# A quarter token tile moved from dense products to gathers, a whole tile likewise, and the reordering of background work that goes with it

## The chip, the cores and the metric

The kernel runs on one core of one Trainium2 chip. The metric is the device time of one execution in microseconds (us); the smaller, the better. Before the change three runs gave 3330.73, 3334.25 and 3336.74 us, median 3334.25 us.

## What is computed

One decoder block over 1024 tokens of width 1024, in float32. The first sub-layer (pooling mixer and forgetting attention, gated) is not touched. The second one is a product-key mixture of 16384 single-neuron experts; its reference, cut to what matters:

```python
q = einsum('bsd,dk->bsk', h, w_query)            # 8 heads, two halves of 128
s1, i1 = top_k(scores of half 0, 16); s2, i2 = top_k(scores of half 1, 16)
top_s, sel = top_k(s1[..., :, None] + s2[..., None, :], 16)
idx = (i1 * 128 + i2)[sel]; gates = softmax(top_s)   # 8 x 16 experts a token
a = gelu(einsum('cd,chkd->chk', x, expert_u[idx])) * gates
out = einsum('chk,chkd->cd', a, expert_v[idx])
```

Each token so uses 128 of the 16384 experts: 128 rows of `expert_u` and 128 rows of `expert_v`, 1024 floats each.

## The kernel before

The 1024 tokens are eight tiles of 128. The first sub-layer, the query products and the top-k of the halves run in three phases of 512, 256 and 256 tokens (`PHASES`, L26; `phase`, L481). In each phase TensorE (PE) has a stream of matmuls, and `tick` (L62) lets a list of background generators (`bg["todo"]`) advance beside it: each matmul group earns credit in us times a rate (`RATES`, L41), and each `yield` of a generator costs what it says.

The experts are done in two ways.

- **Dense** (tiles 1 to 5, `DT0`, `DT1`, L27): all 16384 experts are computed for these 640 tokens. `choose` (L810) finds a token's 128 experts and gates on VectorE (DVE); `gates` (L943) spreads them into a full matrix of gates in DRAM, with one-hot products on PE (`G`, L985) in 32 steps a tile; `dense_experts` (L1002) then runs over 16 groups of 1024 experts. In a group, eight `up` steps (L1018) make 128 experts each for two halves of `NH` = 320 tokens, 24 matmuls a half (8 slices of the width times three, `mm3`, L278, high and low parts of the operands); Gelu, times the gates, split into `ah` and `al`. Eight `down` steps (L1037) multiply by `expert_v` in the same way and add into `accT`. So the stage has 16 x 16 weights of 512 KB. Each is loaded on SP's queue into `wr` (two buffers), rounded to `wh` on ScalarE (ACT) and its remainder `wl` is made on GpSimd (POOL) (`load_w`, L242). There are three `wh`/`wl` pairs in this stage (`W["n"]` = 2 and `W["m"]` = 1).
- **Gathered** (tiles 0, 6 and 7, `experts`, L907): 128 indirect DMAs from POOL fetch, for each of the 128 tokens on the partitions, row k of `expert_u` (512 KB a gather); DVE makes the dot products (L917). Then 128 gathers of `expert_v`, which DVE adds with their weights into `acc` (L927). The operands `h2` and `acc` are in PSUM. Five buffers `g` go round (`g_row`, L894). These generators run in the background of the dense stage, each gather costing `GSTEP` = 1.46 of credit. What is left when the products end is emitted by `drain()` (L1088).

The kernel is not run in the order of its text: the tile framework replays it against its own model of time and writes each engine's list of instructions (`schedule_with_timeline_sim`, L1190). On the chip each engine and queue then runs its list in order. The gathers stay in order among themselves (`keep_in_program_order`, L904).

Of the kernel before, what the change touches and what calls it, by code (L numbers as in the profile page):

```python
# [17 lines left out]
D = 1024  # L18
# [8 lines left out]
DT0, DT1 = 1, 6  # L27
ND = (DT1 - DT0) * 128
# [12 lines left out]
RATES = (0.92, 0.95, 0.74, 0.95)  # L41
# [5 lines left out]
def block_kernel(ctx: ExitStack, tc: tile.TileContext, I, out, dbg=None):  # L47
# [173 lines left out]
    def rstd(ss):  # L221
        nc.vector.tensor_add(ss[:, 2:3], ss[:, 0:1], ss[:, 1:2])
        nc.scalar.activation(ss[:, 3:4], ss[:, 2:3], AF.Sqrt, scale=1.0 / D, bias=epsc)
        nc.vector.reciprocal(ss[:, 3:4], ss[:, 3:4])
        return ss[:, 3:4]
# [166 lines left out]
    def head2(c):  # L392
# [17 lines left out]
        fhl = c.big.tile([48, n], R, name="fhl", tag="fhl", bufs=1)  # L410
# [70 lines left out]
    def phase(c, nxt):  # L481
# [230 lines left out]
        if p == 2:  # L712
            bg["todo"].insert(0, gates(W["gb"], DT1 - 1))
# [32 lines left out]
        dl = [i for i in range(NQ) if DT0 <= qb0 + i < DT1]  # L746
        gl = [i for i in range(NQ) if i not in dl]
        if dl:
            T = slice(dl[0] * 128, dl[-1] * 128 + 128)
            o = (qb0 + dl[0] - DT0) * 128  # L750
            mv(h2dT[0][:, :, o:o + len(dl) * 128], h2h[:, :, T])
            mv(h2dT[1][:, :, o:o + len(dl) * 128], h2l[:, :, T])
            per = D // n
            for b, v in enumerate(tiles):
                mv(x1dT[:, b * per:(b + 1) * per, o:o + len(dl) * 128], v[:, :, T])
# [54 lines left out]
    def choose(tt, mv_, mx_):  # L810
        yield 0.0
        dense = DT0 <= tt < DT1
# [54 lines left out]
        gt = sel.tile([128, PH, 16], F, name="gate", tag="gated" if dense else f"gate{tt}", bufs=1)  # L867
# [7 lines left out]
        if not dense or (dbg and "idx" in dbg):  # L875
            ix = sel.tile([128, 128], I32, name=f"idx{tt}")
# [4 lines left out]
        if dense:  # L881
            tr = W["gb"].tile([128, 3, 128], F, name="pairT", tag="pairT", bufs=DT1 - DT0)
# [5 lines left out]
        if dbg and "idx" in dbg:  # L888
            nc.sync.dma_start(dbg["idx"][tt * 128:(tt + 1) * 128], ix)
            nc.sync.dma_start(dbg["gate"][tt * 128:(tt + 1) * 128], gate[tt])  # L890

    X = {"i": 0, "p": None}
# [13 lines left out]

    def experts(tt):  # L907
        yield 0.0
        row = g_row("row")
        nc.sync.dma_start(row, h2d[tt])  # L910
        h2 = X["ps"].tile([128, D], F, name="h2", tag="gx", bufs=1)
        nc.scalar.activation(h2, row, AF.Copy)
        dots = gp.tile([128, 128], F, name="dots", tag="dots", bufs=1)
# [5 lines left out]
        nc.vector.tensor_mul(dots, dots, gate[tt])  # L919
        acc = X["ps"].tile([128, D], F, name="acc", tag="gx", bufs=1)  # L920
        for k in range(128):
            yield GSTEP
            g = gather(I["peer_v"], idx[tt][:, k:k + 1])
# [8 lines left out]
        r1, r2 = g_row("r1"), g_row("r2")  # L932
        nc.sync.dma_start(r1, x1d[tt])
        nc.sync.dma_start(r2, I["final_g"].partition_broadcast(128))
        nc.vector.tensor_tensor(r0, r0, r1, op=OP.add)
        ss = cst.tile([128, 4], F, name="ss", tag="ssg", bufs=2)
        nc.scalar.activation(r1, r0, AF.Square, accum_out=ss[:, 3:4])
        nc.scalar.activation(ss[:, 3:4], ss[:, 3:4], AF.Sqrt, scale=1.0 / D, bias=epsc)
        nc.vector.reciprocal(ss[:, 3:4], ss[:, 3:4])
        nc.vector.scalar_tensor_tensor(r0, r0, ss[:, 3:4], r2, op0=OP.mult, op1=OP.mult)  # L940
        nc.sync.dma_start(out[tt * 128:(tt + 1) * 128, :], r0)

    def gates(gb, tt):  # L943
# [35 lines left out]
        def use(q, o1, o2):  # L979
# [8 lines left out]
            if r == 3:  # L988
                nc.sync.dma_start(Gd[:, :, (tt - DT0) * 8 + c, :].rearrange("g p x -> p g x"),
# [3 lines left out]
        for q in range(32):  # L993
# [8 lines left out]
    def dense_experts():  # L1002
# [3 lines left out]
        W["x"], W["m"], W["i"] = dd, 1, 2  # L1006
# [78 lines left out]
        for i in range(DT1 - DT0):  # L1085
            finish_dense(i, rows, fg[:, 0])
# [107 lines left out]
```

## Time and profile before

| what | us |
|---|---|
| median of three runs | 3334.25 |
| the profiled execution, its own time | 3331.02 |
| its span, first to last instruction | 3329.3 |
| PE busy in the span | 3123.0 |
| DVE busy | 2440.7 |
| POOL busy | 1754.0 |
| ACT busy | 1266.9 |

The mean granted clock of TensorE was 0.977 of full speed. All times below are from the start of the span. The dense stage begins at about 1490 us and its last product ends at about 3312 us; the three phases lie before it. PE's busy time is a sum over overlapping matmuls that is cut to their union, so a busy PE may still issue more slowly than it could; the pace of matmuls in a stretch is its length over their number.

### The profile page before, as it was taken

How to read it: one execution, taken by the hardware profiler on the slowest of the kernel's cores; microseconds unless marked ns; L12 is line 12 of the kernel's file. 1: busy time of each engine (PE TensorE's matmuls, PEld its weight loads, DVE VectorE, ACT ScalarE, POOL GpSimd, SP SyncE). 2: the span in 40 equal slices, each digit the busy share in tenths (PEclk: the TensorE clock that was granted, in tenths of full speed). 3: DMA queues.
4: the chain of work that ended last, by engine and by line, in shares of the span. 5: the costliest groups of instructions: out<-in, count | busy, mean ns of one | idle time of the engine just before them, and what ended most of it. 6: DMA issues, size and time to landing. Idle time of an engine off the chain costs nothing.

```text
span 3329.3 us, 56918 instructions
## 1 busy us (share of the span) xinstructions
PE 3123.0 (94%) x20912; PEld 2982.7 (90%) x20912; DVE 2440.7 (73%) x5520; ACT 1266.9 (38%) x2405; POOL 1754.0 (53%) x1328
## 2 busy tenths in 40 slices
PE   6999889888888899889999999999999999999998
PEld 4778778778778889789999999999999999999998
DVE  5764557998947987669977877686778767767774
ACT  4555543346542666532222322332232222222222
POOL 1233233014411323326677777687778767877782
PEclk9999999899999999999999999999999999999999
DMA  8987787777788778888899999899999989999994
GB/s 321 354 300 260 274 290 285 243 228 232 235 280 301 234 254 280 274 315 310 278 343 348 329 331 339 312 349 336 333 337 335 335 318 348 335 336 337 348 323 149
DMA packets 379990, 1004.60 MB, mean 302 GB/s; under 512 B 34896, under 2 KB 147136, under 8 KB 379584
## 3 DMA queue, kind: packets, MB, share of 16 engines
q1 hardware_dynamic: 269120, 598.26, 52.3%
q0 software_dynamic: 110592, 402.70, 33.1%
q8 instruction: 166, 2.72, 0.3%
q14 instruction: 112, 0.92, 0.1%
HBM read 851.25 MB, written 149.58 MB: 301 GB/s over the span
## 4 chain that ended last, share of the span: by engine, by line
PE 59%; DVE 11%; DMA 3%; ACT 1%; issue 1%; POOL 0%; SPq 0%; DVEq 0%; ACTq 0%; POOLq 0%
PE z L281 10%; PE z L279 10%; PE z L280 10%; PE oT L280 8%; PE oT L279 8%; PE oT L281 8%; PE G L985 3%; DVE g L917 2%; DVE cand L860 1%; DVE o L975 1%; DMA wl<-w_queryl 1%; DVE pk L864 1%; DMA wr<-w_queryl 1%; DVE mx L585 1%; ACT Gb L986 1%
## 5 line engine op out<-in xcount | busy, mean ns | idle before, releaser
L233 POOL TENSOR_TENSOR wl<-wr,wh 128x1024 fp32r<-128x1024 f32 x320 | 777.0, 2429 | 550.4 <-ACT wh L232 510.2
L232 ACT ACTIVATE wh<-wr 128x1024 fp32r<-128x1024 f32 x325 | 344.0, 1059 | 973.4 <-PE oT L280 429.5
L279 PE MATMUL z<-h2x,wh 128*128 128x320 f32 x2048 | 636.4, 311 | 7.7 <-DVE al L233 5.8
L281 PE MATMUL z<-h2x,wl 128*128 128x320 f32 x2048 | 635.5, 311 | 3.1 <-POOL wl L233 3.1
L280 PE MATMUL z<-h2x,wh 128*128 128x320 f32 x2048 | 635.6, 310 | 0.0
L280 PE MATMUL oT<-al,wh 128*128 128x320 f32 x2048 | 632.8, 309 | 0.4 <-DVE al L233 0.3
L279 PE MATMUL oT<-ah,wh 128*128 128x320 f32 x2048 | 631.9, 310 | 0.7 <-ACT ah L232 0.7
L281 PE MATMUL oT<-ah,wl 128*128 128x320 f32 x2048 | 632.3, 309 | 0.2 <-POOL wl L233 0.2
L917 DVE SCALAR_TENSOR_TENSOR g<-g,h 128x1024 f32<-128x1024 f32 x384 | 461.0, 1215 | 77.5 <-DMA g<-peer_u,idx 75.9
L927 DVE SCALAR_TENSOR_TENSOR acc<-g,dots,acc 128x1024 f32<-128x1024 f32 x381 | 489.2, 1284 | 22.6 <-DMA g<-peer_v,idx 18.8
L902 POOL DMA_INDIRECT g<-peer_u,idx x384 | 363.2, 946 | 163.3 <-DVE g L917 70.3
L902 POOL DMA_INDIRECT g<-peer_v,idx x384 | 361.3, 941 | 114.8 <-issue 50.5
L279 PEld LDWEIGHTS z<-h2x,wh 128*128 128x128 f32 x2048 | 386.6, 189 | 8.9 <-DVE al L233 6.6
L281 PEld LDWEIGHTS z<-h2x,wl 128*128 128x128 f32 x2048 | 386.3, 189 | 3.5 <-POOL wl L233 3.5
L280 PEld LDWEIGHTS z<-h2x,wh 128*128 128x128 f32 x2048 | 386.5, 189 | 0.0
L279 PEld LDWEIGHTS oT<-ah,wh 128*128 128x128 f32 x2048 | 384.1, 188 | 1.4 <-ACT ah L232 1.3
L280 PEld LDWEIGHTS oT<-al,wh 128*128 128x128 f32 x2048 | 384.4, 188 | 0.9 <-DVE al L233 0.9
L281 PEld LDWEIGHTS oT<-ah,wl 128*128 128x128 f32 x2048 | 384.3, 188 | 0.5 <-POOL wl L233 0.5
L973 POOL TENSOR_TENSOR o<-hi,lo 128x512 f32<-128x512 f32 x160 | 199.9, 1252 | 300.0 <-PE G L985 245.4
L279 PE MATMUL z<-hTh,wh 128*128 128x256 f32 (+1 forms) x840 | 290.2, 350 | 29.6 <-issue 12.3
L1050 DVE TENSOR_TENSOR accT<-accT,oT 128x320 f32<-128x320 f32 x240 | 116.5, 487 | 233.6 <-PE oT L281 232.8
L280 PE MATMUL z<-hTl,wh 128*128 128x256 f32 (+1 forms) x840 | 285.0, 339 | 1.3 <-DVE hTl L233 1.3
(286 smaller groups left out, 6094.5 us busy)
## 6 DMA issues: line engine op xcount, KB each, us to landing
wr<-ut SPq DMA_DIRECT2D x128, 512.0 KB
wr<-vt SPq DMA_DIRECT2D x128, 512.0 KB
Gd<-Gb SPq DMA_DIRECT2D x40, 1024.0 KB
Gg<-Gd SPq DMA_DIRECT2D x64, 640.0 KB
wh<-w_inh SPq DMA_DIRECT2D x60, 512.0 KB
wl<-w_inl SPq DMA_DIRECT2D x60, 512.0 KB
wm<-w_mod SPq DMA_DIRECT2D x48, 512.0 KB
wr<-w_in SPq DMA_DIRECT2D x45, 512.0 KB
```

Of the source, the lines that this page charges most:

```text
L232: nc.scalar.activation(hi, src, AF.Copy)
L233: eng_lo.tensor_tensor(lo, src, hi.bitcast(F), op=OP.subtract)
L279: nc.tensor.matmul(ps, ah, bh, start=start, stop=False)
L280: nc.tensor.matmul(ps, ah, bl, start=False, stop=False)
L281: nc.tensor.matmul(ps, al, bh, start=False, stop=stop)
L585: nc.vector.tensor_reduce(mx[:, x:x + 1], sp[:, :w], axis=AX.X, op=OP.max, negate=True)
L902: d = nc.gpsimd.indirect_dma_start(out=g, out_offset=None, in_=table, in_offset=bass.IndirectOffsetOnAxis(ap=col, axis=0))
L917: nc.vector.scalar_tensor_tensor(g, g, 1.0, h2, op0=OP.mult, op1=OP.mult, accum_out=dots[:, k:k + 1])
L927: nc.vector.scalar_tensor_tensor(acc, g, dots[:, k:k + 1], acc, op0=OP.mult, op1=OP.add)
L973: nc.gpsimd.tensor_tensor(o2, hi[:, X, :, None].to_broadcast([128, 4, 8, 16]), lo[:, X, None, :].to_broadcast([128, 4, 8, 16]), op=OP.mult)
L985: nc.tensor.matmul(ps[:, b * 128:(b + 1) * 128], o1[:, b], o2[:, b], start=True, stop=True)
L1050: nc.vector.tensor_tensor(acc[:, c, T], acc[:, c, T], o, op=OP.add)
```

## The change

The tokens 32 to 639 become dense (608, halves of 304 columns). Tile 5 is gathered as a whole now, and of tile 0 the first 32 tokens alone (`HT`): their 32 x 128 pairs of token and expert are laid out as 4 x 32 partitions by 32 columns, so that this quarter costs 32 gathers of `expert_u` and 32 of `expert_v`; three additions over partition blocks fold the result. Gathers: 2 x 32 + 3 x 256 = 832, where there were 768. `gates` makes 24 steps for tile 0 and 32 for tiles 1 to 4, 152 where there were 160. The phases run `choose` for tiles 0 to 4; that of tiles 5, 6 and 7 runs beside the dense products, where it was 6 and 7. There are four `wh`/`wl` pairs, and the rate beside the dense products is 0.865 in place of 0.74. Tile 5 needs rows `x1d` and `h2d` in DRAM, made in the second phase.

```diff
 PHASES = ((0, 512), (512, 256), (768, 256))
-DT0, DT1 = 1, 6
-ND = (DT1 - DT0) * 128
+
+DA, DB = 32, 640
+HT, DT1 = 0, 5
+HK = 32
+ND = DB - DA
...
-RATES = (0.92, 0.95, 0.74, 0.95)
+RATES = (0.92, 0.95, 0.865, 0.95)
...
-        fhl = c.big.tile([48, n], R, name="fhl", tag="fhl", bufs=1)
+        fhl = c.tile("plh", 1, R)
...
         if p == 2:
-            bg["todo"].insert(0, gates(W["gb"], DT1 - 1))
             bg["rate"] = RATES[3]
...
-        dense = DT0 <= tt < DT1
+        dense = tt < DT1
+        gathered = tt == HT or not dense
...
     def experts(tt):
         yield 0.0
+
+        n, K = (HK, HK) if tt == HT else (128, 128)
         row = g_row("row")
-        nc.sync.dma_start(row, h2d[tt])
+        ix, gt = idx[tt], gate[tt]
+        if tt == HT:
+            ix = sel.tile([128, HK], I32, name="ixh", tag="ixh", bufs=1)
+            gt = sel.tile([128, HK], F, name="gth", tag="gth", bufs=1)
+            for b in range(128 // HK):
+                to, c = slice(b * HK, b * HK + HK), slice(b * HK, b * HK + HK)
+                nc.sync.dma_start(ix[to], idx[tt][:HK, c])
+                nc.sync.dma_start(gt[to], gate[tt][:HK, c])
+                nc.sync.dma_start(row[to], h2d[tt][:HK])
+        else:
+            nc.sync.dma_start(row, h2d[tt])
...
-        for k in range(128):
+        for k in range(K):
             yield GSTEP
-            g = gather(I["peer_u"], idx[tt][:, k:k + 1])
+            g = gather(I["peer_u"], ix[:, k:k + 1])
...
+        if tt == HT:
+            for b in range(1, 128 // HK):
+                nc.sync.dma_start(r1[:n], r0[b * n:b * n + n])
+                nc.vector.tensor_tensor(r0[:n], r0[:n], r1[:n], op=OP.add)
+                r1 = g_row("r1")
...
-        for q in range(32):
+        for q in range(DA // 4 if tt == HT else 0, 32):
             yield GC
...
-        W["x"], W["m"], W["i"] = dd, 1, 2
+        W["x"], W["m"], W["i"] = dd, 2, 3
...
-    late = [experts(tt) for tt in range(DT0)]
-    bg["todo"] = ch[:DT0] + [f for i in range(DT0, 4) for f in (ch[i], gates(gb, i))]
+    early = [experts(HT)]
+    bg["todo"] = [f for i in range(4) for f in (ch[i], gates(gb, i))]
...
-    bg["todo"] += [f for i in range(4, DT1) for f in (ch[i - 4], gates(gb, i))][:-1]
+    bg["todo"] += [ch[0], gates(gb, 4)]
+    late = ch[1:]
...
-    bg["todo"] = late + [f for i, tt in enumerate(range(DT1, 8)) for f in (ch[i], experts(tt))]
+    bg["todo"] = early + [f for i, tt in enumerate(range(DT1, 8)) for f in ((late + ch)[i], experts(tt))]
     bg["rate"] = RATES[2]
     dense_experts()
```

Since the framework writes the engines' lists, three places show what the change makes of them.

POOL, the end of its list, before: `wl` is the remainder of one dense weight (256 of them in the stage), `g` a gather, `x4` that a row stands four times.

```order
L233 TENSOR_TENSOR wl<-wr,wh 128x1024
L902 DMA g<-peer_v,idx_29506 128x1024 x3
L233 TENSOR_TENSOR wl<-wr,wh 128x1024
L902 DMA g<-peer_v,idx_29506 128x1024 x4
L233 TENSOR_TENSOR wl<-wr,wh 128x1024
L902 DMA g<-peer_v,idx_29506 128x1024 x2
L233 TENSOR_TENSOR wl<-wr,wh 128x1024 x7
```

The same place in the changed kernel:

```order
L237 TENSOR_TENSOR wl<-wr,wh 128x1024
L903 DMA g<-peer_v,idx_30120 128x1024 x3
L237 TENSOR_TENSOR wl<-wr,wh 128x1024
L903 DMA g<-peer_v,idx_30120 128x1024 x2
L237 TENSOR_TENSOR wl<-wr,wh 128x1024
L903 DMA g<-peer_v,idx_30120 128x1024 x116
```

Before, the last gather stood ahead of the last seven weights; now 116 gathers stand behind the last weight.

DVE, behind the last product of the dense stage, before: L1050 and L1052 take the last half tile of products, then come the final norms of the dense tokens.

```order
L1050 TENSOR_TENSOR accT<-accT,oT 128x320
L1052 SCALAR_TENSOR_TENSOR accT<-accT,modc,h2x_35394 128x320
L222 TENSOR_TENSOR ss<-ss 128x1 x2
L224 RECIPROCAL ss<-ss 128x1
L1068 SCALAR_TENSOR_TENSOR Gg<-pt,ss,h2x_35395 128x512 x2
```

The changed kernel; `acc<-g,dots,acc` is the sum of one gather of `expert_v`, and the last four rows finish the last gathered tile:

```order
L1073 TENSOR_TENSOR accT<-accT,oT 128x304
L943 SCALAR_TENSOR_TENSOR acc<-g,dots,acc 128x1024
L1075 SCALAR_TENSOR_TENSOR accT<-accT,modc,h2x_35567 128x304
...
L1091 SCALAR_TENSOR_TENSOR h2x_35568<-z,ss,h2x_35568 96x512 x2
L943 SCALAR_TENSOR_TENSOR acc<-g,dots,acc 128x1024 x97
L947 TENSOR_TENSOR r_35281<-acc,r_35281 128x1024
L958 TENSOR_TENSOR r_35281<-r_35281,r_35284 128x1024
L962 RECIPROCAL ss<-ss 128x1
L963 SCALAR_TENSOR_TENSOR r_35281<-r_35281,ss,r_35285 128x1024
```

Behind the last dense product there was no gathered sum; now there are 9 between the rows left out and 97 in a row.

PE, the query products of the third phase (`h2h`, `h2l`), before: `G` are the one-hot products of `gates`.

```order
L985 MATMUL G<-o_16893,o_16892 128x128 x4
L279 MATMUL z<-h2h,wh 128x256 x2
L280 MATMUL z<-h2l,wh 128x256
L281 MATMUL z<-h2h,wl 128x256
L280 MATMUL z<-h2l,wh 128x256
L281 MATMUL z<-h2h,wl 128x256
L279 MATMUL z<-h2h,wh 128x256 x2
L985 MATMUL G<-o_16904,o_16903 128x128 x4
```

In the changed kernel the last `G` of the list stands ahead of the output projection of that phase (`yTh`):

```order
L1008 MATMUL G<-o_14631,o_14630 128x128 x4
L642 MATMUL o<-th,vv 128x256
L643 MATMUL o<-tl,vv 128x256
...
L642 MATMUL o<-th,vv 128x128
L643 MATMUL o<-tl,vv 128x128
L283 MATMUL z<-yTh,wh 128x256
```

So no one-hot product is left beside the output projection and the query products of the third phase.

## Rows read from the trace of the kernel before

**Rows 1.** The page, span and busy time of each engine.
```profile
span 3329.3 us, 56918 instructions
PE 3123.0 (94%) x20912; PEld 2982.7 (90%) x20912; DVE 2440.7 (73%) x5520; ACT 1266.9 (38%) x2405; POOL 1754.0 (53%) x1328
```
**Rows 2.** The chain of work that ended last, share by engine.
```profile
PE 59%; DVE 11%; DMA 3%; ACT 1%; issue 1%; POOL 0%; SPq 0%; DVEq 0%; ACTq 0%; POOLq 0%
```
**Rows 3.** Windows: length, busy us and instructions by engine, granted clock, DMA share, GB/s.
```profile
900.00:1490.00 590.00, 519.56 (x4067) 493.27 (x4066) 430.15 (x1302) 311.63 (x629) 166.46 (x150) 0.97 0.84 275
1490.00:1700.00 210.00, 199.22 (x1308) 196.31 (x1309) 199.41 (x540) 60.07 (x102) 143.14 (x107) 0.97 0.84 295
1700.00:3240.00 1540.00, 1540.00 (x10502) 1540.00 (x10501) 1128.18 (x1664) 418.63 (x672) 1176.99 (x906) 1.00 0.93 335
3240.00:3312.00 72.00, 72.00 (x494) 72.00 (x493) 36.61 (x55) 15.22 (x22) 23.52 (x13) 1.00 0.45 166
3312.00:3330.00 18.00, 5.50 (x39) 4.15 (x36) 9.16 (x22) 7.36 (x25) 0.00 (x0) 0.67 0.37 147
```
**Rows 4.** The page's groups: one of the six dense matmul groups, x2048 each.
```profile
L279 PE MATMUL z<-h2x,wh 128*128 128x320 f32 x2048 | 636.4, 311 | 7.7 <-DVE al L233 5.8
```
**Rows 5.** Timeline of PE, 256 columns in the third phase: start, duration.
```profile
1333.28 0.28 PE L279 MATMUL z<-hTh,wh 128*128 128x256 f32 x1
...
1334.93 0.29 PE L639 MATMUL o<-tl,vv 128*128 128x256 f32 x1
```
**Rows 6.** The page's groups: DVE on one gather.
```profile
L917 DVE SCALAR_TENSOR_TENSOR g<-g,h 128x1024 f32<-128x1024 f32 x384 | 461.0, 1215 | 77.5 <-DMA g<-peer_u,idx 75.9
L927 DVE SCALAR_TENSOR_TENSOR acc<-g,dots,acc 128x1024 f32<-128x1024 f32 x381 | 489.2, 1284 | 22.6 <-DMA g<-peer_v,idx 18.8
```
**Rows 7.** Timeline of DVE, two gathered sums back to back.
```profile
1907.76 2.61 DVE L927 SCALAR_TENSOR_TENSOR acc<-g,dots,acc 128x1024 f32<-128x1024 f32 x2
```
**Rows 8.** Timeline of POOL, three gathers back to back.
```profile
2013.04 0.95 POOL L902 DMA_INDIRECT g<-peer_v,idx  x1
...
2015.53 0.94 POOL L902 DMA_INDIRECT g<-peer_v,idx  x1 [0.30 <-DVE al L233]
```
**Rows 9.** The page's DMA queues: the gathers' queue (packets, MB, share).
```profile
q0 software_dynamic: 110592, 402.70, 33.1%
```
**Rows 10.** The tile g from 1540 to 3270 us: landing of a gather.
```profile
DMA to landing us min/median/max: 4.2/6.1/14.1
```
**Rows 11.** What PE waited for, 900 to 1490 us: total, times, longest.
```profile
PE G L985 <- POOL o L973: 8.7, 11, 2.1
PE G L985 <- ACT Gb L986: 8.5, 6, 3.7
PE G L985 <- issue: 4.6, 5, 1.4
```
**Rows 12.** Timeline of PE: eight one-hot passes (four products).
```profile
1420.62 1.05 PE L985 MATMUL G<-o,o 128*128 128x128 f32 x8
```
**Rows 13.** Groups of DVE, 1490 to 1715 us (L860, L864: choose).
```profile
L917 DVE SCALAR_TENSOR_TENSOR g<-g,h 128x1024 f32<-128x1024 f32 x83 | 100.2, 1212 | 7.9 <-DMA g<-peer_u,idx 7.9
L860 DVE SCALAR_TENSOR_TENSOR cand<-pk 128x128 f32<-128x128 f32 x64 | 26.3, 547 | 0.0
L864 DVE TENSOR_REDUCE pk<-cand 128x128 f32<-128x1024 f32 x8 | 9.7, 1211 | 0.0
```
**Rows 14.** A window of 20 us early in the dense stage, columns as Rows 3.
```profile
1640.00:1660.00 20.00, 14.19 (x85) 13.40 (x84) 20.00 (x41) 5.74 (x12) 12.66 (x11) 0.89 0.84 287
```
**Rows 15.** Timeline of DVE: end of a gathered tile, end of the dense tokens.
```profile
3256.23 1.22 DVE L931 TENSOR_TENSOR r<-acc,r 128x1024 f32<-128x1024 f32 x1
...
3263.06 1.28 DVE L940 SCALAR_TENSOR_TENSOR r<-r,ss,r 128x1024 f32<-128x1024 f32 x1
...
3312.35 0.55 DVE L1052 SCALAR_TENSOR_TENSOR accT<-accT,modc,h2x 128x320 f32<-128x320 f32 x1
...
3324.23 1.41 DVE L1068 SCALAR_TENSOR_TENSOR Gg<-z,ss,h2x 128x512 f32<-128x512 f32 x2
```

More of the change, by code (lines that the diff above doesn't have):

```diff
@@ L745, in phase @@
         z0, = to_T(c, x1, rsb, sc2, sh2, h2h, h2l, [("w_query", 0)])
[L746 to L752, printed above, removed]
+        lo, hi = max(t0, DA), min(t0 + n, DB)
+        gl = [i for i in range(NQ) if not DA <= t0 + i * 128 <= DB - 128]
+        if lo < hi:
+            T = slice(lo - t0, hi - t0)
+            O = slice(lo - DA, hi - DA)
+            mv(h2dT[0][:, :, O], h2h[:, :, T])
+            mv(h2dT[1][:, :, O], h2l[:, :, T])
             per = D // n
             for b, v in enumerate(tiles):
-                mv(x1dT[:, b * per:(b + 1) * per, o:o + len(dl) * 128], v[:, :, T])
+                mv(x1dT[:, b * per:(b + 1) * per, O], v[:, :, T])
         if gl:
@@ L866, in choose @@
             nc.vector.tensor_add(dst, dst, pf)
-        gt = sel.tile([128, PH, 16], F, name="gate", tag="gated" if dense else f"gate{tt}", bufs=1)
+        gt = sel.tile([128, PH, 16], F, name="gate", tag="gate" if gathered else "gated", bufs=3 if gathered else 1)
         nc.vector.tensor_tensor(gt, ts, ts[:, :, 0:1].to_broadcast([128, PH, 16]), op=OP.subtract)
@@ L874, in choose @@
         gf = gt.rearrange("p h k -> p (h k)")
-        if not dense or (dbg and "idx" in dbg):
-            ix = sel.tile([128, 128], I32, name=f"idx{tt}")
+        if gathered:
+            ix = sel.tile([128, 128], I32, name=f"idx{tt}", tag="idx", bufs=3)
             nc.vector.scalar_tensor_tensor(ix, w0, 128.0, w1, op0=OP.mult, op1=OP.add)
@@ L881, in choose @@
         if dense:
-            tr = W["gb"].tile([128, 3, 128], F, name="pairT", tag="pairT", bufs=DT1 - DT0)
+            tr = W["gb"].tile([128, 3, 128], F, name="pairT", tag="pairT", bufs=DT1)
             pt = pt_tile()
@@ L887, in choose @@
             pairT[tt] = tr
[L888 to L892, printed above, removed]
+    X = {"i": 0, "p": None, "ps": None}
     def g_row(name):
@@ L1054, in down, with finish_dense @@
             tick(24 * ND * 0.00043)
-        def finish_dense(i, rows, fg):
+        def finish_dense(i, yt, fg):
             ps = [f() for f in ((pt_tile, pt_tile), (z_tile, z_tile), (s_tile, s_tile))[i % 3]]
             ss = cst.tile([128, 4], F, name="ss", tag="ssd", bufs=2)
-            yt = rows[:, i * D:i * D + D]
+            T = slice(i * 128, min(i * 128 + 128, ND))
+            n = T.stop - T.start
             hs = (slice(0, 512), slice(512, 1024))
@@ L1084, in dense_experts @@
                 down(gr, i)
-        for i in range(DT1 - DT0):
-            finish_dense(i, rows, fg[:, 0])
+        for i in range((ND + 127) // 128):
+            finish_dense(i, rows[:, i * D:i * D + D] if i < 4 else fg[:, 1], fg[:, 0])
         W["m"], X["p"] = 0, None
```

50 lines of the change are left out of this document (27 added, 23 removed).

## The prediction

> **What bounds the kernel now.** I read the page first [rows 1]: PE is busy for 3123.0 of 3329.3 us, and the reader is to see that no other engine comes near. The chain [rows 2] agrees: 59% of the span is PE's, 11% DVE's. The windows [rows 3] then cut the span by stage. In the phases (900 to 1490 us) PE is idle for 70 of 590 us. In the dense stage it is busy without a gap from 1700 to 3312 us, at a granted clock of 1.00, which is the 2.4 GHz level, while DVE is busy for 73% (1128 of 1540) and POOL for 76%; the DMA engines are at 0.93. Only at its start, 1490 to 1700 us, does DVE bind: it is busy for 199 of 210 us. From 3240 us on the DMA share falls to 0.45: the gathers are done, and the last products run alone. So a dense product less is worth its full time, and gathers cost nothing as long as they fit beside the products. Whether they still fit is not in these rows but in the order of the changed kernel, and there lies the decision.
>
> All sums are made against the profiled execution, span 3329.3 us, own time 3331.0; the median of the runs is 3334.25, and I add the difference to that. A change of under 0.2% (6.7 us) could not be told from none here.
>
> **Part by part.**
>
> *Narrower products: -90.* The matmuls of the dense stage number 6 x 2048 [rows 4] and stay as many. From 1700 to 3240 us 10502 were issued in 1540 us [rows 3], 146.6 ns each, for 320 columns. Does this shrink with the columns? In the third phase 14 matmuls of 256 columns took from 1333.28 to 1334.93 us [rows 5], 117.9 ns each. Per column that is 0.460 ns against 0.458: no fixed share. So 304 columns take 139.3 ns, and 12288 x 7.33 ns = 90 us. A line through the two points gives 88; I take 90.
>
> The Trainium skill, "TensorE: Matmul & The Clock Gate", section "Back-to-back issue gap", gives columns / 2.4 GHz plus 2.5 ns for a lone stream, 135.8 ns at 320. The trace differs by 11 ns a matmul. By that rule the estimate of the saving would be 82 us, and the whole sum 8 us higher.
>
> *Gathers: 64 more, and what the order makes of them: +143.* The plan: at rate 0.865 a group of 16 weights earns 16 x 24 x 608 x 0.00043 x 0.865 = 87 of credit, or 59 gathers at 1.46; before it was 54. At that plan all 832 would be emitted before the last group ends. The written order does not follow it. Counted on POOL's list, the full groups before held 45 to 51 gathers between their weights, and now they hold 41 to 48: per us of products 50 / 112.6 = 0.44 and 47.5 / 107.0 = 0.44. The framework's own model of time admits no more, so a higher rate buys nothing, and the shorter stage holds fewer. 116 gathers stand behind the last weight. On DVE 106 sums (9 and 97) stand behind the last dense product. Those cannot run earlier, since each list runs in order, so they come after PE has ended.
>
> What does one of these cost? By DVE: two in a row take 2.61 us with 1.28 for the second [rows 6, 7], so 1.33 us from one to the next, since each reads the `acc` that the former wrote. By POOL: 2.49 us for two steps [rows 8], 1.25. By the DMA engines: 33.1% of 3329.3 us over 768 gathers [rows 1, 9] is 1.435 us each, measured beside other traffic. By the five buffers: landing 4.2 at best, 6.1 in the median [rows 10], plus 1.28 on DVE and some 0.3 until POOL goes on, over five: 1.16 to 1.54. The largest of each end bounds it: 1.33 to 1.54. I take 1.40, nearest to the row of DVE, since the weights' traffic is gone by then. 106 x 1.40 = 148 us. The ten norms of the dense tokens (0.7 each, [rows 15]) fit between.
>
> Then the last tile is finished: 8.1 us from its first addition to its last product [rows 15], and 3.7 from DVE's last instruction to the end of the span [rows 1, 15]. So the end comes 148 + 8 + 4 = 160 us after the last dense sum. Before it came 16.4 us after it (3312.9 to 3329.3). The difference is +143, with ends of +136 and +158.
>
> *`choose` of tile 5 moved into the dense stage: +12.* DVE binds at its start [rows 3], and in one window PE lost 6 of 20 us to it [rows 14]. Here DVE's list is the evidence: before, the first two groups held two `choose` and 92 gathered sums, now three `choose` and 72. A `choose` costs at least half of L860 and L864 (18 us), at most half of what DVE does there besides the L917 sums, (199 - 100) / 2 = 50 us [rows 3, 13]; I take 40, since many short instructions belong to it. 20 sums less save 24 us [rows 6]. So DVE has about 16 us more to do while the products there last 11 us less. 27 us could go to PE; part of it is taken up by the free PSUM tiles between PE and DVE. I take 12, ends 0 and 27.
>
> *Phases: -15.* `choose` of tile 5 and eight steps of `gates` leave. 32 products of `G` are 64 passes at (1.05 - 0.28) / 7 = 0.11 us [rows 12], 0.28 being the time of one pass alone as in [rows 5]: 7 us of PE. PE waited for `gates` for 21.8 us between 900 and 1490 us [rows 11]; the order shows no `G` beside the last output and query products any more, and I take 8 of these 21.8. DVE gets up to 50 us free, but in a stretch where it was busy for 430 of 590 us [rows 3], so I cost that at nothing. Against it stand tile 5's extra rows (8 transposes, four transfers of 512 KB). Ends: a loss of 5, or a gain of 45.
>
> *At nothing:* the fourth `wh`/`wl` pair (PE waits for `wl` and `wh` for almost nothing already [rows 4]; the cover is PE's own pace, and without it one late weight costs about 3 us), the small transfers for tile 0 (SP's list has them in the second phase), the shared `plh` tile, the three folding additions (DVE, beside products).
>
> Sum: -90 + 143 + 12 - 15 = +50. The span becomes 3379 us, the median 3384.
>
> **The rivals.**
>
> *The buffers hold the tail.* If landing stays at its median, a gather costs 1.54 us and the tail 163: 3399 us. For it: five buffers, a median of 6.1. Against: that median is measured with the weights in the queues. With DVE's 27 us on top it is 3414. Chance 0.15.
>
> *Columns don't pay in full.* Mechanism: part of a matmul's pace doesn't depend on its columns. If that were a tenth of the 146.6 ns, a tenth of the 90 us would stay, and the time would be 3393. For it speaks nothing but caution; the equal cost per column at 256 and 320 [rows 3, 5] speaks against. Chance 0.05. The Trainium skill's page named above would have it so, with its 2.5 ns and its 8 us.
>
> *Not slower: the phases give it all back.* Mechanism: DVE, relieved of a `choose` and of 8 steps, lets PE run through. The place is 900 to 1490 us, where PE is idle for 70 us [rows 3]. It decides from 58 us on, in place of the 15: then the time is 3341 us; at 65 us it is 3334, no change. Only 21.8 us of that idle time are waits for `gates` [rows 11], and the DVE work that stays is still there. Chance 0.05, of which 0.03 is no change.
>
> *The change doesn't do what it says.* In part this is my forecast: the gathers don't all lie beside the products, whatever the rate. If the chip were to place them otherwise than the lists, the tail would vanish and the time be 3334 - 90 + 12 - 15 = 3241. Lists run in order: chance 0.01.
>
> **How the numbers follow.** Forecast, some 3384 us: 0.74. Its own range, with the ends of the terms partly offsetting, is 3345 to 3408: below, the 30 more from the phases and some of the 12 of DVE and the 7 of the tail; above, 15 from DVE and 10 from the tail. Buffers 0.15, columns 0.05, not slower 0.06. The range 3342 to 3411 takes in the first three but for the worst of the buffers, and leaves out the cases that are not slower. Slower 0.94, same 0.03, faster 0.03.
>
> **What would show it.** Right: the last matmul with 304 columns near 3210 us, then some 150 us with PE empty, DVE on L943, POOL on gathers about 1.4 us apart; 10502 matmuls in about 1463 us. Right for the phases: the first dense product some 15 us earlier. Wrong: gathers in the stage at 54 a group, or PE gaps spread over the stage (the DMA engines or DVE the bound), or a tail under 100 us.

## The result, and the profile after

The changed kernel takes 3429.54 us in the median of four runs (3426.68 to 3442.64), where the kernel before took 3332.49 (3328.83 to 3336.74) beside it: a ratio of 1.0298 (of the means), with a 95% interval of 1.0276 to 1.0321. It is slower by 97 us. The direction and the main mechanism, a tail of gathers behind the products, are those of the prediction, but the time lies 45 us above the 3384 and 18 above the end of the range.

The profiled execution has a span of 3428.9 us, 99.6 more than before. Two lines of its page, busy times and the chain by engine, answer to [rows 1, 2]:

```profile
PE 3036.1 (89%) x20856; PEld 2893.3 (84%) x20856; DVE 2529.5 (74%) x5616; ACT 1264.5 (37%) x2413; POOL 1806.7 (53%) x1383
PE 65%; DVE 14%; DMA 10%; issue 4%; ACT 3%; POOL 2%; SPq 1%; POOLq 0%; DVEq 0%; ACTq 0%
```

PE is busy for 87 us less, and the span is longer all the same. The windows by stage, columns as in [rows 3], and the timeline of PE at the first and at the last dense product (start, duration) show where the time lies:

```profile
900.00:1490.00 590.00, 510.39 (x3889) 483.06 (x3889) 401.18 (x1267) 295.70 (x614) 150.39 (x129) 0.95 0.81 266
1498.00:1700.00 202.00, 183.47 (x1238) 180.25 (x1237) 196.31 (x507) 62.06 (x104) 131.22 (x93) 0.96 0.77 266
1700.00:3200.00 1500.00, 1494.64 (x10716) 1493.53 (x10715) 1098.52 (x1757) 425.77 (x692) 1145.67 (x869) 1.00 0.92 332
2900.00:3200.00 300.00, 300.00 (x2157) 300.00 (x2156) 213.30 (x399) 90.07 (x148) 233.07 (x178) 1.00 0.92 334
3262.00:3415.00 153.00, 0.00 (x0) 0.00 (x0) 129.51 (x107) 0.70 (x3) 89.91 (x96) 0.50 0.95 346
```

```profile
1497.65 0.41 PE L283 MATMUL z<-h2x,wh 128*128 128x304 f32 x1 [1.27 <-ACT wh L236]
...
3246.37 0.30 PE L285 MATMUL oT<-ah,wl 128*128 128x304 f32 x1
```

The same two products in the kernel before:

```profile
1489.86 0.42 PE L279 MATMUL z<-h2x,wh 128*128 128x320 f32 x1 [1.35 <-ACT wh L232]
...
3311.48 0.31 PE L281 MATMUL oT<-ah,wl 128*128 128x320 f32 x1
```

Three stretches make up the 99.6 us.

| stretch | before | after | change | forecast |
|---|---|---|---|---|
| start to first dense product | 1489.9 | 1497.7 | +7.8 | -15 |
| first to last dense product | 1821.9 | 1749.0 | -72.9 | -78 (-90 and +12) |
| last dense product to the end | 17.5 | 182.3 | +164.7 | +143 |

In the first 202 us of the stage PE is idle for 18.5 us. The waits of PE there (in total, times, longest), and from the page the product group that answers to [rows 4] and the gathers' queue that answers to [rows 9]:

```profile
PE z L283 <- DVE al L237: 11.6, 6, 2.7
PE oT L284 <- DVE al L237: 4.3, 3, 2.3
```

```profile
L283 PE MATMUL z<-h2x,wh 128*128 128x304 f32 x2048 | 622.2, 304 | 13.3 <-DVE al L237 11.6
...
q0 software_dynamic: 119808, 436.26, 34.9%
```

Nearly all that the group waits for in the whole stage is DVE's `al` in those 202 us; from 1700 us on the products run on without a gap worth naming.

Behind the last product PE has nothing to do, its granted clock is 0.50 (1.2 GHz, the lower level), and what runs are gathers and their sums. The groups there, 3262 to 3415 us, the waits, and the landing of a gather (its median in us, the last number):

```profile
L943 DVE SCALAR_TENSOR_TENSOR acc<-g,dots,acc 128x1024 f32<-128x1024 f32 x100 | 128.9, 1289 | 23.5 <-DMA g<-peer_v,idx 20.7 <-DVE acc L943 0.3
L903 POOL DMA_INDIRECT g<-peer_v,idx x96 | 89.9, 937 | 60.7 <-DVE acc L943 45.9 <-DMA g<-peer_v,idx 7.8 <-issue 3.7
```

```profile
POOL g L903 <- DVE acc L943: 45.9, 78, 1.6
DVE acc L943 <- DMA g<-peer_v,idx: 20.7, 35, 1.2
```

```profile
g<-peer_v,idx POOLq DMA_INDIRECT x96, 6.0
```

100 sums took 153 us, 1.53 each. DVE waits for the DMA that fills its buffer, POOL waits for the sum that frees one: a ring of five that goes round. From the last product to the last sum (3419.4) there are 107 sums in 172.8 us, 1.61 each; the first twenty, with the norms and the five stores of the dense tokens between them, were slower, 2.16 each for ten and 1.65 for the next ten.

### The profile page after: what moved, and what is told of

Read it like the earlier page. It is cut to its first block, busy times and chain, and to the rows that moved or that the text cites. A ratio compares the mean times of both kernels' runs of the same rounds, so it can differ in the third digit from the quotient of the medians.

```text
span 3428.9 us, 57001 instructions
## 1 busy us (share of the span) xinstructions
PE 3036.1 (89%) x20856; PEld 2893.3 (84%) x20856; DVE 2529.5 (74%) x5616; ACT 1264.5 (37%) x2413; POOL 1806.7 (53%) x1383
## 4 chain that ended last, share of the span: by engine, by line
PE 65%; DVE 14%; DMA 10%; issue 4%; ACT 3%; POOL 2%; SPq 1%; POOLq 0%; DVEq 0%; ACTq 0%
PE z L283 12%; PE z L285 11%; PE z L284 11%; PE oT L284 8%; PE oT L283 8%; PE oT L285 8%; PE G L1008 3%; DMA g<-peer_v,idx 3%; DVE cand L864 2%; DVE acc L943 1%; DMA g<-peer_u,idx 1%; DMA wl<-w_queryl 1%; DVE g L933 1%; DVE pk L868 1%; DVE o L998 1%
## 5 line engine op out<-in xcount | busy, mean ns | idle before, releaser
L283 PE MATMUL z<-h2x,wh 128*128 128x304 f32 x2048 | 622.2, 304 | 13.3 <-DVE al L237 11.6
L284 PE MATMUL oT<-al,wh 128*128 128x304 f32 x2048 | 619.5, 303 | 8.0 <-DVE al L237 8.0
L284 PE MATMUL z<-h2x,wh 128*128 128x304 f32 x2048 | 620.9, 303 | 0.0
L283 PE MATMUL oT<-ah,wh 128*128 128x304 f32 x2048 | 616.2, 302 | 3.3 <-ACT ah L236 3.3
L285 PE MATMUL z<-h2x,wl 128*128 128x304 f32 x2048 | 618.1, 302 | 0.4 <-POOL wl L237 0.4
L285 PE MATMUL oT<-ah,wl 128*128 128x304 f32 x2048 | 615.4, 301 | 0.0
L943 DVE SCALAR_TENSOR_TENSOR acc<-g,dots,acc 128x1024 f32<-128x1024 f32 x412 | 529.4, 1285 | 38.2 <-DMA g<-peer_v,idx 32.0
L933 DVE SCALAR_TENSOR_TENSOR g<-g,h 128x1024 f32<-128x1024 f32 x416 | 497.9, 1215 | 49.1 <-DMA g<-peer_u,idx 42.8
L285 PE MATMUL z<-hTh,wl 128*128 128x256 f32 (+1 forms) x840 | 284.9, 339 | 1.9 <-DMA wl<-w_inl 1.4
```

What stands on the lines that cost most here:

```text
L283: nc.tensor.matmul(ps, ah, bh, start=start, stop=False)
L284: nc.tensor.matmul(ps, ah, bl, start=False, stop=False)
L285: nc.tensor.matmul(ps, al, bh, start=False, stop=stop)
L943: nc.vector.scalar_tensor_tensor(acc, g, dots[:, k:k + 1], acc, op0=OP.mult, op1=OP.add)
```

## The experiments

Three theories were under test. **B**: the written order, and with it the five buffers, put the gathers behind the products, and room in the order would bring them back. **D**: the DMA path has no room for them beside the weights. **P**: behind the products the ring of buffers sets the price of a gather. The starts and ends of products below are read from the timeline of PE, as above. A time without a range is that of one run; the four runs of the changed kernel lie within 16 us of each other, so what a smaller difference in time says is read from the stages.

**1. The rate alone, twice.**

```diff
-RATES = (0.92, 0.95, 0.865, 0.95)
+RATES = (0.92, 0.95, 0.74, 0.95)
```

> The changed kernel with the background rate back at 0.74. In POOL's order 117 gathers stand behind the last weight, against 116 in the changed kernel. Theory B (the framework's order, with its five gather buffers, sets how many gathers lie beside the products, not the rate): 3430 us, within 7, the last product within 5 us of 3247. Theory D (the DMA engines are at their ceiling of some 340 GB/s beside the products already, so that a gather costs its bytes wherever it stands): the same 3430, since the bytes stay. Rival R (the higher rate crowds the start of the dense stage and takes 20 us from PE there): the first products run freer, 3405 to 3415.

Measured: 3501.61 us. The last product ends at 3249, as expected, but a gather behind it cost 2.25 us. Since that was neither theory, it was run again:

> The kernel with the rate of 0.74 once more, in several executions, since its gathers behind the products took 2.25 us each where 1.5 to 1.6 was expected, with the DMA engines at 0.74. Theory K (the price belongs to the program, its order or its addresses): every run near 3500, 2.2 us a gather. Theory S (it belongs to the execution): the runs are near 3430, or some of them.

Measured: 3502.19 us in the median of four runs (3497.06 to 3505.80), ratio 1.0505 (1.0479 to 1.0530). Theory K holds, it belongs to the program. Groups and window of 3300 to 3480 us:

```profile
L943 DVE SCALAR_TENSOR_TENSOR acc<-g,dots,acc 128x1024 f32<-128x1024 f32 x80 | 103.1, 1289 | 77.2 <-DMA g<-peer_v,idx 77.1
```

```profile
3300.00:3480.00 180.00, 0.00 (x0) 0.00 (x0) 102.85 (x80) 0.00 (x0) 74.73 (x80) 0.50 0.74 232
```

The code has a reason. After the last product the kernel sets `X["p"] = None` and then calls `drain()`; `g_row` then takes only the `GBUFS` = 3 buffers outside the dense stage's pool. What the low rate has left to `drain()` goes round three buffers; the rate of 0.865 emits all gathers ahead of that line. The next run keeps the pool until `drain()` is done.

**2. The low rate with five buffers to the end.**

```diff
-        W["m"], X["p"] = 0, None
+        W["m"] = 0
         drain()
+        X["p"] = None
```

> The rate of 0.74 once more, but what is left when the products end goes on with all five gather buffers: the text of the kernel gives back the two in the dense stage's pool before it emits the rest, so that at the low rate, where some 100 gathers are left to that place, three buffers went round behind the products (at the rate of 0.865 all are emitted before it). Theory K3 (three buffers in place of five made the 2.25 us a gather): 1.5 to 1.6 us a gather, the DMA engines at 0.94 or more again, 3425 to 3440 us. Rival (something else in the order at the low rate): 3490 or more.

Measured: 3437.59 us, and in the window from 3270 to 3420 us 98 sums in 150 us, 1.53 each. Theory K3 holds. So the higher rate is worth 72 us in this kernel (3502 to 3430), and some 65 of them (3502 to 3438) are not more gathers beside the products, but two buffers behind them. The 8 us that are left lie within the spread of the changed kernel's runs.

**3. Three weight pairs.**

```diff
-        W["x"], W["m"], W["i"] = dd, 2, 3
+        W["x"], W["m"], W["i"] = dd, 1, 2
```

> The changed kernel with three weight pairs in place of four. In POOL's order 113 gathers stand behind the last weight (116). Theories B and D: the pair is worth nothing, 3420 to 3435 us; PE's waits for wl and wh stay under 5 us in sum. Rival (the fourth pair is what carries PE over late weights): PE waits for wl or wh by 10 us or more, and the time is 3440 or more.

Measured: 3432.13 us. The fourth pair is worth nothing that shows.

**4. Seven gather buffers** in place of the fourth pair: the edit of experiment 3, and

```diff
-GMORE = 2
+GMORE = 4
```

> The changed kernel with three weight pairs and seven gather buffers in place of five (the SBUF of the pair goes to them). The order then holds 56 gathers beside a full group of 16 weights (47) and none behind the last weight. Theory B (only the order kept the gathers behind the products): the tail of 165 us goes and the products keep 139 ns, 3265 us, within 10. Theory D (the DMA engines are the bound): 626 MB have to be moved from 1497 us on, whatever the order, at 335 to 346 GB/s 1810 to 1869 us, so the end is at 3315 to 3375 us, PE gets gaps over the whole stage, and its pace is 143 ns a matmul or more. Theory P (only the buffers' round trip is at fault) is B here.

Measured: 3420.75 us (3418.47 to 3422.51), ratio 1.0267 (1.0243 to 1.0291). All 832 gathers lie beside the products now, the last product ends at 3400, and almost nothing is won. Theory B falls. D's time is missed by 46 us as well, since it took the DMA engines to be full to the end. Windows, and what PE waits for from 1700 to 3400 us (us in total, times, longest):

```profile
1700.00:2900.00 1200.00, 1141.75 (x7990) 1130.56 (x7989) 897.71 (x1404) 311.02 (x506) 923.90 (x720) 0.98 0.94 342
2900.00:3400.00 500.00, 456.92 (x3096) 444.02 (x3094) 357.58 (x526) 117.76 (x200) 351.63 (x278) 0.97 0.86 317
```

```profile
PE oT L285 <- POOL wl L237: 47.7, 16, 7.6
PE z L283 <- ACT wh L236: 17.9, 21, 1.4
PE z L285 <- POOL wl L237: 17.2, 28, 2.8
PE oT L283 <- ACT wh L236: 15.5, 14, 1.9
```

PE issues 7990 matmuls in 1200 us, 150.2 ns each where the changed kernel has 139 to 140, and it waits for weights, 98 us in sum. The DMA engines move 342 GB/s, where it was 332 in the changed kernel.

The stage takes 1894.6 us, 146 more than in the changed kernel. PE stands still for 101 us of the 1700 in these two windows. Most of the rest goes with its granted clock, 0.98 and 0.97 where the changed kernel had 1.00: over 1200 and 500 us that is worth 24 and 15 us of PE at full speed. What the weights themselves wait for shows on ACT, which makes `wh` out of a load. Its waits for loads from 1700 to 2900 us, with seven buffers and then in the changed kernel:

```profile
ACT wh L236 <- DMA wr<-vt: 319.0, 51, 16.4
ACT wh L236 <- DMA wr<-ut: 76.9, 14, 12.2
```

```profile
ACT wh L236 <- DMA wr<-vt: 149.5, 25, 13.0
ACT wh L236 <- DMA wr<-ut: 50.4, 8, 9.3
```

ACT waits 396 us for loads in place of 200, and PE then waits for what ACT and POOL make of them.

**5. Half of the weights' loads left out**, with seven buffers.

```diff
-    def load_w(src, eng=None):
-        wr = W["p"].tile([128, 8, 128], F, name="wr", tag="wr", bufs=2)
-        nc.sync.dma_start(wr, src)
+    def load_w(src, eng=None, again=False):
+        if not again:
+            W["wr"] = W["p"].tile([128, 8, 128], F, name="wr", tag="wr", bufs=2)
+            nc.sync.dma_start(W["wr"], src)
+        wr = W["wr"]
...
-            wh, wl = load_w(I["ut"][e])
+            wh, wl = load_w(I["ut"][e], None, e % 2 == 1)
...
-            wh, wl = load_w(I["vt"][gr * 8 + c], nc.gpsimd)
+            wh, wl = load_w(I["vt"][gr * 8 + c], nc.gpsimd, c % 2 == 1)
```

> The kernel with seven gather buffers, but only every second dense weight is loaded; the next one is made from the same load, with all roundings, remainders and products kept (half of the experts are so left out of the result). The order keeps 55 gathers a group and none behind. 67 MB less go over the DMA engines. Theory D (in the run with seven buffers the DMA engines held up PE): PE runs at 139 to 141 ns a matmul again, the dense stage lasts 1750 to 1775 us in place of 1895, the time is 3270 to 3300. Rival V (DVE or POOL, which have the same to do, held it up): the stage keeps more than half of its loss, 3350 or more.

Measured: 3282.49 us; the dense stage lasts 1759 us. Two windows:

```profile
1700.00:2900.00 1200.00, 1188.18 (x8484) 1186.86 (x8484) 983.80 (x1564) 337.83 (x550) 991.12 (x779) 0.99 0.92 330
2900.00:3200.00 300.00, 300.00 (x2157) 300.00 (x2156) 246.01 (x338) 82.44 (x135) 256.08 (x202) 1.00 0.94 337
```

All gathers run beside the products and PE is back at 139.1 ns from 2900 us on (300 / 2157; 141.4 up to there), with DVE busier than in experiment 4 (82% from 2900 us on), and ACT waits for loads for 8 us in place of 396. So neither DVE nor POOL held up PE there; the weights' loads did. Theory D holds against V. But the edit halves two things, the bytes of the loads and how often one of the two load buffers has to come free, so it does not tell which of them was short.

**6. Eight gather buffers** and two weight pairs (`dd, 0, 1`, `GMORE = 5`, and the pool kept through `drain()`).

> Eight gather buffers and two weight pairs; the order holds 60 gathers beside a full group of weights (56 with seven buffers, 47 in the changed kernel) and none behind the last. With seven, the stage took 1895 us at 342 GB/s, although gathers alone reach 394 with as many buffers. Theory D (weights and gathers together do not pass some 345 GB/s on the DMA engines): the same bytes, the same end, 3405 to 3425, with more PE gaps earlier and fewer later. Theory Q (seven buffers were too few beside the products too, and more requests under way bring up the rate): 360 GB/s or more in the stage, 3340 to 3380. Rival L (weights come later the more gathers are queued ahead of them): PE's waits for wh and wl grow and nothing comes back later, 3440 or more.

Measured: 3444.25 us, in none of the ranges of D and Q and in that of L. Three windows:

```profile
1700.00:2900.00 1200.00, 1126.20 (x7771) 1101.71 (x7771) 901.33 (x1400) 309.35 (x509) 912.63 (x716) 0.98 0.92 338
2900.00:3300.00 400.00, 374.15 (x2571) 365.12 (x2571) 301.01 (x446) 92.04 (x151) 316.48 (x253) 0.97 0.97 357
3330.00:3420.00 90.00, 85.13 (x592) 84.39 (x591) 35.73 (x61) 24.12 (x37) 30.41 (x14) 0.96 0.37 136
```

Up to 2900 us the eighth buffer brings no higher rate (338 against 342), so Q falls. From 3330 us on the gathers are over and the DMA engines nearly idle while PE still has 90 us to go; that is what D's estimate lacked. L's own sign, growing waits for weights, is hardly there: 103 us against 98. Whether some 340 GB/s is a limit of the engines for this mix of transfers (357 in one stretch), or follows from the two load buffers that a weight has to pass, is not settled (see experiment 12).

**7. Seven buffers behind the products.** First with `RATES[2]` 0.70 in experiment 4's kernel:

> Seven gather buffers and three pairs as in the run with seven buffers, but a rate of 0.70, so that 139 gathers stand behind the last weight again (116 in the changed kernel). It measures the price of a gather in the tail, 1.61 us in the changed kernel. Theory P (five buffers: landing 6 us, the sum 1.28 and POOL's turn make 8 us, over five 1.6): with seven it is DVE's 1.33. Theory D (512 KB at 340 GB/s): 1.53 to 1.6 as before, landing grows to 8 us or more, the DMA engines at 0.94 or more.

Measured: 3568.32 us, 2.2 us a gather, which could not tell P from D, since `drain()` ran with three buffers here too. Then with the edit of experiment 2:

> Seven gather buffers, rate 0.70, with all seven kept for the 139 gathers that are left behind the last weight. It was meant to be measured before, but there only three went round. Three buffers gave 2.22 us a gather, so a round trip of 6.7 us; five would give 1.33 by that, and gave 1.5 to 1.6. Theory D (the DMA engines bind from 340 GB/s on): with seven still 1.50 to 1.58 us, 0.94 or more of the DMA engines, landing longer. Theory P (the buffers' round trip binds still): 1.33 us, DVE's own.

Measured: 3449.78 us. Groups, waits and window from 3270 to 3420 us:

```profile
L943 DVE SCALAR_TENSOR_TENSOR acc<-g,dots,acc 128x1024 f32<-128x1024 f32 x112 | 144.4, 1290 | 4.5 <-DMA g<-peer_v,idx 0.4 <-DVE acc L943 0.3
```

```profile
POOL g L903 <- DVE acc L943: 43.1, 102, 2.1
DVE acc L943 <- DMA g<-peer_v,idx: 0.4, 1, 0.4
```

```profile
3270.00:3420.00 150.00, 0.00 (x0) 0.00 (x0) 145.49 (x115) 0.00 (x0) 104.25 (x111) 0.50 1.01 391
```

DVE no longer waits for a gather; 112 sums and two norms fill the 150 us, 1.32 us from one sum to the next. Theory P holds behind the products: 2.25 us with three buffers, 1.53 with five, 1.32 with seven, and 232, 346 and 391 GB/s. Landing fits it: a median of 5.1 us with three buffers (the low rate, 3300 to 3480 us), 6.0 with five (the changed kernel, above) and 5.9 with seven (3280 to 3410 us). With 1.29 for the sum and some 0.3 until POOL goes on, over the number of buffers, that makes 2.2, 1.5 and 1.1 us, and with seven the sum itself takes longer than that. What was 0.95 of the DMA engines in the changed kernel's last stretch was no limit of theirs.

**8. The quarter tile's gathers left out.**

```diff
-    early = [experts(HT)]
+    early = []
```

> The changed kernel without the 64 gathers of the quarter tile: 608 dense tokens, 768 gathers (rows 0 to 31 of the output are left out). In POOL's order 45 gathers stand behind the last weight (116). Theory D with the order as it stands: the products as in the changed kernel (first at 1498, 1749 us long), then some 10 sums at 2.0 and 35 at 1.53, and 9 us to finish: 3325 to 3338, no gain over the kernel before although 92 us of products are gone. Rival (the gathers that are not added find room beside the shorter products): 3275 to 3300.

Measured: 3311.15 us, 14 below the range. The products took 1741 us, and 37 sums came behind them, where 107 had. 70 sums at 1.53 make 107 us and the products 8, together 115 of the 118 us that it gives back (3429.5 to 3311.2). The tail shrank by more than 64: the order held 45 gathers behind the last weight, where it held 116. With no gathers in their place the narrower products would have been a gain of 19 us over the kernel before (3330.4 beside it); the gathers that replace them undo it.

**9. The gates of tile 4 back at their old place.**

```diff
         if p == 2:
+            bg["todo"].insert(0, gates(W["gb"], DT1 - 1))
             bg["rate"] = RATES[3]
...
-    bg["todo"] += [ch[0], gates(gb, 4)]
+    bg["todo"] += [ch[0]]
```

> The changed kernel with the gates of tile 4 put back to where the last gates stood before, beside the output and query products of the third phase. Theory P (there the weights' loads bind, so that this work was free, and in the stretch before it, it is not): the output products of the third phase begin 10 to 16 us earlier than the 1372 of the changed kernel, and the first dense product comes at 1482 to 1490 us in place of 1498. Rival W (the work costs the same wherever it stands): the first dense product stays at 1495 to 1505. What follows after it is the changed kernel's, 3415 to 3435 in all, since a gather behind the products costs 1.5 to 1.6.

Measured: 3430.07 us. PE's timeline has the first and the last output product of the third phase and the first dense product, first of the changed kernel, then of this one:

```profile
1372.24 0.39 PE L283 MATMUL z<-yTh,wh 128*128 128x256 f32 x1 [1.78 <-DMA yTh<-yd]
...
1418.29 0.28 PE L285 MATMUL z<-yTh,wr 128*128 128x256 f32 x1
```

```profile
1356.03 0.36 PE L283 MATMUL z<-yTh,wh 128*128 128x256 f32 x1 [0.51 <-DMA yTh<-yd]
...
1419.78 0.28 PE L285 MATMUL z<-yTh,wr 128*128 128x256 f32 x1
...
1499.54 0.41 PE L283 MATMUL z<-h2x,wh 128*128 128x304 f32 x1 [0.97 <-ACT wh L236]
```

The output products begin 16 us earlier and end where they did. W holds: the gates cost the same at either place.

**10. No rows of tile 5.** The first sub-layer's values of tile 5 are not written to `x1d` and `h2d`; its gathered part reads those of tile 6.

```diff
-        gl = [i for i in range(NQ) if not DA <= t0 + i * 128 <= DB - 128]
+        gl = [i for i in range(NQ) if not DA <= t0 + i * 128 <= DB - 128 and qb0 + i != DT1]
...
-            nc.sync.dma_start(row, h2d[tt])
+            nc.sync.dma_start(row, h2d[max(tt, 6)])
```

> The changed kernel without the extra rows of tile 5 in the second phase (eight transposes, their copies, additions and four transfers); tile 5 is then fed from the rows of tile 6, so its gathers fetch the same rows of the tables but its values are left out. Theory P (these rows hold up the second phase's query products): those end 10 to 13 us earlier than 1051 and the first dense product comes at 1483 to 1490 us. Rival (the prediction: they are cheap): the query products end within 4 us of 1051, the first dense product comes at 1495 to 1502.

Measured: 3417.14 us. The last query product of the second phase, the changed kernel and then this one with its first dense product:

```profile
1051.02 0.28 PE L285 MATMUL z<-h2h,wl 128*128 128x256 f32 x1
```

```profile
1038.96 0.28 PE L285 MATMUL z<-h2h,wl 128*128 128x256 f32 x1
...
1486.99 0.41 PE L283 MATMUL z<-h2x,wh 128*128 128x304 f32 x1 [1.04 <-ACT wh L236]
```

In the kernel before it was:

```profile
1038.32 0.28 PE L281 MATMUL z<-h2h,wl 128*128 128x256 f32 x1
```

The rows cost 12 us there, nearly the whole delay against the kernel before, and 11 at the first dense product. (That start lies between 1496 and 1507 us in the runs whose phases are the changed kernel's, so a few us of it may be chance; the 1039 lies clear of the other runs' 1049 to 1057.)

**11. The choice of tile 5 back in the phases.**

```diff
-    bg["todo"] += [ch[0], gates(gb, 4)]
-    late = ch[1:]
+    bg["todo"] += [ch[0], gates(gb, 4), ch[1]]
+    late = [iter(())]
```

> The changed kernel with the choice of tile 5 back in the phases, where it was before the change. In POOL's order 107 gathers stand behind the last weight (116). Theory M (in the dense stage's start, where DVE binds, it costs PE some 12 us): from first to last dense product 1735 to 1743 us in place of 1749; nine gathers less behind them, 13 to 15 us; against it, the first dense product comes 5 to 15 us later than 1498. Together 3410 to 3430. Rival H (DVE had room for it at either place): the first product at 1498 within 4, the stage 1749 within 3, and only the nine gathers show, 3415.

Measured: 3415.43 us. First dense product at 1510.9 (+13), products 1732 us long (-17, a little more than M had it), and 11 us less behind them. M holds.

**12. What the runs so far make together.** Three load buffers (the third in the dense stage's pool), two weight pairs, seven gather buffers, kept to the end:

```diff
-        wr = W["p"].tile([128, 8, 128], F, name="wr", tag="wr", bufs=2)
+        W["r"] = (W["r"] + 1) % (2 + W["k"])
+        wp, n = (W["p"], 2) if W["r"] < 2 else (W["x"], W["k"])
+        wr = wp.tile([128, 8, 128], F, name="wr", tag="wr", bufs=n)
...
+        W["k"] = 1
```

> Three buffers for the load of a weight (two before), two weight pairs, seven gather buffers, all seven kept behind the products. The order holds 47 gathers a group again and leaves 95 behind the last weight (116). Theory D with the price of seven buffers: products as in the changed kernel (first at 1498 to 1507, 1740 to 1750 us long), then some 100 sums, the first ten at 1.5 to 2.0, the rest at 1.33, and 9 us to finish: 3385 to 3405. Rival (the price behind the products stays 1.53): 3405 to 3425.

Measured: 3402.22 us (3396.43 to 3410.71), ratio 1.0208 (1.0181 to 1.0235); products 1747 us long, 96 sums behind them. The stage and the last 100 us of gathers:

```profile
1700.00:3200.00 1500.00, 1493.22 (x10698) 1491.61 (x10697) 1081.15 (x1749) 425.95 (x691) 1154.58 (x879) 1.00 0.92 335
3280.00:3380.00 100.00, 0.00 (x0) 0.00 (x0) 96.41 (x75) 0.00 (x0) 70.19 (x75) 0.50 1.01 399
```

75 sums in 100 us: the price behind the products is 1.33, as D with seven buffers had it. And from 1700 to 2900 us ACT waits for weights' loads for 6 us, where it was 200 in the changed kernel, at nearly the same number of gathers (521 and 512 issued) and 335 GB/s. So with a third load buffer that wait is gone; in experiments 4 and 6, with fewer pairs and more gather buffers but two load buffers, it was not. Whether PE would then also run on beside the 56 gathers a group of experiment 4 was not run, since the order held 47 here. With the choice of tile 5 moved as in experiment 11 besides:

> The kernel with three load buffers and seven gather buffers, and besides the choice of tile 5 back in the phases. The order leaves 87 gathers behind the last weight. By the runs so far: first product at 1505 to 1512, products 1732 to 1742 us long, then 87 to 92 sums at 1.33 with a slower start, and 9 us: 3368 to 3388. It is still slower than the kernel before by every theory here; only if gathers found more room beside the products than the order gives could it come near 3330.

Measured: 3402.92 us, a miss by 15. The first dense product came at 1522.2, 15.6 us later than without the move, and the products took 1745 us, 2 less, where experiment 11 had 17 less. PE idled for 15.8 us before that product, waiting for ACT's first `wh`; it was 11.7 us without the move, and 1.2 in experiments 4 and 6, with two load buffers. Why the products gained nothing here is not shown. No version with all 832 gathers and all weights loaded came near 3332.

## Why the prediction was right and wrong

**What bounds the kernel, and the gathers' place: right.** That a gather costs nothing as long as it fits beside the products, and that the order does not let the 64 more fit, was the step that gave the sign. It forecast 106 sums behind the last product, 9 and 97, and left out the one that stands first in the order shown; 107 came.

**Why they don't fit: wrong in part.** The prediction put it on the framework's model of time alone. Experiment 4 gives the order the room and gains 9 us, and experiments 4 and 5 show what stands in the way: with more gathers beside the products the weights' loads come too late for PE, and with half of the loads they do not. From 1700 to 2900 us no run moved more than 342 GB/s. Whether the engines' throughput is what is short, or the way of a load through its two buffers, stays open (experiments 5, 6 and 12). Either way tokens were moved from PE to transfers that, in this program, had no free room for them. The prediction named the 0.93 of [rows 3] and drew nothing from it; the share alone would not have proved it (last section), but it was the place to look.

**Narrower products, -90: right.** 2157 matmuls from 2900 to 3200 us are 139.1 ns each; 139.3 was forecast. With +12 for the choice of tile 5 the stage should have shortened by 78 us; it did by 72.9, a miss of 5. The place was right, the first 202 us with DVE's `al`, and experiment 11 bears out the mechanism.

**The tail, +143: the price of one gather was mis-sized.** The step that failed is "I take 1.40, nearest to the row of DVE, since the weights' traffic is gone by then". Between 1.33 and 1.54 the buffers held the upper end: 1.53, and 1.61 with the slower start, where the norms and stores of the dense tokens lie; the prediction had put the norms between the sums at no cost. This is the rival "the buffers hold the tail" at 1.54, which had 0.15. Landing stayed at 6.0 us without the weights' traffic, against the 6.1 of [rows 10]. DVE's price comes only with seven buffers (experiments 7, 12). Of the 49.6 us between the forecast sum (+50) and the span (+99.6), 22 are here.

**Phases, -15: wrong, +7.8.** The step that failed is "tile 5's extra rows", set against the gains but put at nothing in the sum: they hold up the query products of the second phase by 12 us (experiment 10). And the 8 us of waits for `gates` taken as a gain were none: the three waits of [rows 11], 21.8 us together, make 21.7 in the changed kernel (POOL `o` 5.4, ACT `Gb` 6.0, issue 10.3), PE's idle time from 900 to 1490 us went from 70 to 80, and experiment 9 shows that the last gates cost the same beside the output products as ahead of them. Without the rows the first dense product comes 2.9 us earlier than before the change (1487.0 against 1489.9), so of the 15 us at most some 3 came, and that is within the scatter of this start. 23 us of the miss are here.

**The rate, "a higher rate buys nothing": wrong.** It buys 72 us (experiments 1 and 2). The order's count of gathers a group was read rightly, and it is the same at both rates; what was missed is a line of the program, the two buffers that go back before `drain()`. The forecast itself was not touched by it, since the change has the high rate.

**The range.** Each wrong step came out a little beyond an end that the text had named (1.61 for 1.54; +7.8 for +5). The range left out the two together.

## What to carry to other kernels

Before work is moved from one engine to another, read what the receiver already carries in the stretch where the work will lie: DMA engines that move weights and gathers at some 335 GB/s beside a full PE took 2 to 3% more when pressed (342), and PE then waited for its weights. Work that spills behind the main stage cost its round trip over the number of buffers here (2.25 and 1.53 us), until with seven buffers the busiest engine's own time was longer (1.32), so count the buffers that are live at that place in the program, and not in the stage. A step taken off one part of a pipelined phase is a gain only where the next part does not wait for something else anyway.

## What the hardware showed that was not expected

The share of busy time of the DMA engines is no rate. With gathers alone it was 0.74 at 232 GB/s, 0.95 at 346 and 1.01 at 391 to 399, with three, five and seven buffers. Per gather of 512 KB that is 1.67 us of all engines' time (0.74 x 180 / 80), 1.45 (0.95 x 153 / 100) and 1.35 (1.01 x 150 / 112). Since the bytes are the same, more of that time moves nothing the fewer gathers are under way; no run shows what it is spent on. The 1.435 us of [rows 9] was such a figure too, and no price. The Trainium skill, "Perfetto Trace Analysis", section "Identifying the Most-Contended Engine", warns that occupancy misleads for the 16 DMA engines and wants the utilization of HBM looked at in its place; these three windows agree, for the share goes from 0.74 to 1.01 while the rate goes from 232 to 391 GB/s.

The Trainium skill, "DMA: Bandwidth & Descriptors", section "Where 436 GB/s comes from", puts a core's share of HBM at some 358 GB/s, half of what a stack gives its two cores, and lets transfers between HBM and SBUF be bound by it. This kernel runs on one core, and with seven buffers gathers alone passed that share, with 391 to 399, so it was no bound for them. The mix of weights and gathers stayed below it, at 342 at most from 1700 to 2900 us and 357 in one stretch of 400 us; no run shows whether the two have to do with each other.
